# One of the last stores of a short-sequence attention kernel is cut in two, and three quarters of it are written with an outer dimension of eight

## The chip, the cores and the metric

The kernel runs on one core of a Trainium2 chip. The metric is the device time of one execution in microseconds (us); lower is better. The core has the engines PE (matmul), DVE, ACT and POOL, a queue engine SP, and 16 DMA engines that move data between the device memory and the on-chip memory (SBUF).

## The reference

32 batches with 12 heads each make 384 independent attention problems of 128 rows by 64 columns in float32:

```
scores = scale * np.matmul(q, k.transpose(0, 1, 3, 2))
scores_max = np.max(scores, axis=-1, keepdims=True)
attn = np.exp(scores - scores_max)
attn = attn / (np.sum(attn, axis=-1, keepdims=True) + 1e-8)
return np.matmul(attn, v).astype(np.float32)
```

Each of q, k, v and the output is 12.58 MB.

## The kernel before

The work goes in 24 chunks (`NCH`), numbered 0 to 23, of 16 heads each. A chunk of the output is a tile `o_sb` of 128 partitions, and each partition holds 16 rows (`TQ`) of 64 columns (`D`), that is 1024 floats or 4096 bytes that also lie together in the device memory. A whole chunk is 512 KB. Because a partition is one run of 4096 bytes on both sides, a store of a chunk consists of 128 packets of 4096 bytes; spread over 16 DMA engines that is eight packets, 32 KB, for each engine.

Loads of q, k and v are issued on POOL (lines 58 and 65) and change float32 to bfloat16 on the way, `AHEAD` = 7 chunks ahead of their use. Only chunk 0 of q and k is loaded by SP and ACT and cast by DVE and ACT (lines 78 to 84). For every chunk, in the loop at lines 210 to 229, DVE turns q and k (`turn`), PE makes the scores and ACT their exponentials (`scores`), PE makes the row sums (`denominators`), DVE turns them and takes the reciprocals (`divide`), PE multiplies with v and DVE turns the result into `o_sb` (`outputs`, `finish`), and POOL multiplies with the reciprocals (`scale_rows`, line 183; for the last chunk POOL and DVE take one half each, line 186).

Stores are held back: `held` (lines 194 to 199) is a list, written out by hand, of the chunks that are stored at the end of each step. With `LAG` = 9, chunk c is stored in step c + 9 in the middle of the run. At the end the lists get longer: step 22 stores chunks 18, 19 and 20, and step 23 stores chunks 21, 22 and 23. `store` (lines 189 to 191) is one DMA. Chunks 0 to 20 are issued from ACT's queue, chunks 21 to 23 from SP's queue (line 229). So chunk 20, which the change touches, is the last store that ACT issues, behind those of chunks 18 and 19, and three more stores follow it on SP.

Semaphores and waits are put in by the framework; they are not in the source. Among them are waits of a store for the landing of an earlier store.

Of the kernel before, what the change touches and what calls it, by code (L numbers as in the profile page):

```python
# [10 lines left out]
def kernel(  # L11
# [15 lines left out]
    B, H, S, D = q.shape  # L27
    assert S == 128 and D == 64
    scale = 1.0 / (D ** 0.5)
    TQ = 16  # L30
# [4 lines left out]
    NCH = B * H // 16  # L35
    AHEAD = 7
    LAG = 9

    def runs(x, t):
        return x.rearrange("b h (g t) d -> (b h g) (t d)", t=t).rearrange(  # L40
            "(n p) x -> p n x", p=128)

    qr, kr, vr, orr = runs(q, TQ), runs(k, TQ), runs(v, T), runs(out, TQ)
# [5 lines left out]
    pf = ctx.enter_context(tc.tile_pool(name="pf", bufs=8))  # L49
    po = ctx.enter_context(tc.tile_pool(name="po", bufs=LAG + 3))  # L50
    ps = ctx.enter_context(tc.tile_pool(name="ps", bufs=1, space=bass.MemoryType.PSUM))
# [17 lines left out]
    with tc.manual_schedule():  # L69
# [8 lines left out]
        for src, which, eng, cast in ((qr, 0, nc.sync, nc.vector.tensor_copy),  # L78
# [3 lines left out]
            x = pin.tile([128, TQ, D], bf16, tag="qk"[which] + "_bf", name="qk"[which] + "_bf")  # L82
# [105 lines left out]

        def store(c, eng):
            o_sb, _ = osbs.pop(c)  # L190
            eng.dma_start(out=orr[:, c, :], in_=o_sb.rearrange("p t d -> p (t d)"))

        e = NCH - 1
        held = {c: [c - LAG] if c >= LAG else [] for c in range(e - 4)}
        held[e - 4] = [e - 13, e - 12]
# [14 lines left out]
        for c in range(NCH):  # L210
            todo = shuffles.get(c, [])
            if c < e:
                turn(c + 1, 0)
                turn(c + 1, 1)
            d_ps = denominators(c)
            if c < e:
                scores(c + 1)
            divide(c, d_ps)
            finish(c, 0, outputs(c, 0))
            for x in todo[:len(todo) // 2]:  # L220
                values(*x)
            finish(c, 1, outputs(c, 1))
            for x in todo[len(todo) // 2:]:
                values(*x)
            if c + AHEAD < NCH:
                load(c + AHEAD)
            scale_rows(c)
            for s in held[c]:
                store(s, nc.scalar if s < e - 2 else nc.sync)
# [30 lines left out]
```

## Time and profile before

| | |
|---|---|
| three runs | 130.41, 130.43, 130.69 us, median 130.43 |
| the profiled execution | 130.47 us |
| its span, from the first to the last instruction | 128.6 us |
| busy share of the span: PE, DVE, ACT, POOL | 54%, 67%, 56%, 62% |
| DMA share of the chain that ended last | 58% |
| memory read and written | 37.75 MB and 12.58 MB |
| stores issued by ACT and by SP | 21 and 3, of 512 KB each |

The span leaves out 1.9 us of the profiled execution that lie before the first and after the last instruction. "DMA share" is the mean busy share of the 16 DMA engines in a stretch of time, in which neighbouring packets may overlap a little, so that a full stretch reads as slightly more than 1; 0.50 is what eight busy engines of 16 give. GB/s counts bytes as the packets record them: the casting loads count by what they write, half of what they read.

### The profile page before, as it was taken

How to read it: one execution, taken by the hardware profiler on the slowest of the kernel's cores; microseconds unless marked ns; L12 is line 12 of the kernel's file. 1: busy time of each engine (PE TensorE's matmuls, PEld its weight loads, DVE VectorE, ACT ScalarE, POOL GpSimd, SP SyncE). 2: the span in 40 equal slices, each digit the busy share in tenths (PEclk: the TensorE clock that was granted, in tenths of full speed). 3: DMA queues.
4: the chain of work that ended last, by engine and by line, in shares of the span. 5: the costliest groups of instructions: out<-in, count | busy, mean ns of one | idle time of the engine just before them, and what ended most of it. 6: DMA issues, size and time to landing. Idle time of an engine off the chain costs nothing.

```text
span 128.6 us, 4637 instructions
## 1 busy us (share of the span) xinstructions
PE 69.7 (54%) x2080; PEld 42.7 (33%) x2080; DVE 85.7 (67%) x150; ACT 71.8 (56%) x74; POOL 79.5 (62%) x88
## 2 busy tenths in 40 slices
PE   0036966577546757775636296190976663684000
PEld 0025644444223433443314144050544331552000
DVE  0380398584879678979958669464799997777500
ACT  3216588669658737875774486371757775523000
POOL 6951314235699986998738487808999952355300
PEclk9999999999999977999999959968689998555555
DMA  3999999999999999999999999999999999999982
GB/s 118 312 194 186 210 204 204 209 213 202 216 202 209 207 215 206 207 212 209 283 290 269 221 284 207 286 287 209 287 210 285 287 285 325 389 418 414 419 364 83
DMA packets 16723, 32.27 MB, mean 251 GB/s; under 512 B 1344, under 2 KB 7488, under 8 KB 16704
## 3 DMA queue, kind: packets, MB, share of 16 engines
q0 software_dynamic: 12960, 18.35, 80.1%
q10 hardware_dynamic: 3168, 11.54, 23.0%
q1 hardware_dynamic: 576, 2.10, 4.2%
q8 instruction: 16, 0.26, 0.7%
q14 instruction: 3, 0.02, 0.0%
HBM read 37.75 MB, written 12.58 MB: 391 GB/s over the span
## 4 chain that ended last, share of the span: by engine, by line
DMA 58%; DVE 12%; POOL 11%; PE 6%; issue 4%; ACT 1%; POOLq 0%; DVEq 0%; ACTq 0%
DMA k_bf<-in_k_dram 33%; DMA q_bf<-in_q_dram 11%; DMA v_bf<-in_v_dram 11%; DVE o_sb L178 6%; POOL o_sb L183 4%; POOL v_bf L65 4%; PE s_ps L120 3%; DMA out_dram<-o_sb 3%; DVE kt L109 3%; DVE qt L107 2%; POOL q_bf L58 2%; PE o_ps L159 2%; ACT attn L124 1%; DVE o_sb L186 1%; PE v_ps L139 1%
## 5 line engine op out<-in xcount | busy, mean ns | idle before, releaser
L124 ACT ACTIVATE attn<-s_ps 128x2048 bf16<-128x2048 f32 x24 | 45.1, 1877 | 38.2 <-PE s_ps L120 33.2
L183 POOL TENSOR_TENSOR o_sb<-o_sb,recip 128x1024 f32<-128x1024 f32 x23 | 43.9, 1915 | 8.7 <-DVE o_sb L178 8.5
L178 DVE STREAM_TRANSPOSE o_sb<-o_ps 128x512 f32<-128x512 f32 x48 | 33.1, 711 | 14.3 <-PE o_ps L159 13.2
L139 PE MATMUL v_ps<-v_bf,perm 128*32 128x512 bf16 (+1 forms) x448 | 33.5, 405 | 3.4 <-DMA v_bf<-in_v_dram 3.4
L120 PE MATMUL s_ps<-qt,kt 32*128 32x128 bf16 x768 | 17.2, 232 | 33.1 <-DVE kt L109 33.1
L143 ACT CAST v<-v_ps 128x512 bf16<-128x512 f32 x48 | 26.4, 589 | 2.6 <-PE v_ps L139 2.4
L120 PEld LDWEIGHTS <-kt 32*128 32x128 bf16 x768 | 12.6, 100 | 43.1 <-DVE kt L109 42.5
L159 PE MATMUL o_ps<-attn,v 128*32 128x128 bf16 x768 | 22.4, 245 | 2.7 <-issue 2.7
L58 POOL DMA_DIRECT2D k_bf<-in_k_dram x23 | 12.3, 536 | 15.5 <-DMA v_bf<-in_v_dram 10.8
L171 DVE STREAM_TRANSPOSE dt<-d_ps 128x512 f32<-128x512 f32 x24 | 16.3, 678 | 6.4 <-PE d_ps L149 6.4
L109 DVE STREAM_TRANSPOSE kt<-k_bf 128x512 f32<-128x512 f32 x24 | 16.3, 680 | 5.5 <-DMA k_bf<-in_k_dram 5.4
L159 PEld LDWEIGHTS <-v 128*32 128x32 bf16 x768 | 15.7, 108 | 11.4 <-issue 6.5
L58 POOL DMA_DIRECT2D q_bf<-in_q_dram x23 | 13.5, 585 | 6.4 <-DMA v_bf<-in_v_dram 3.7
L107 DVE STREAM_TRANSPOSE qt<-q_bf 128x512 f32<-128x512 f32 x24 | 16.2, 673 | 1.6 <-DMA q_bf<-in_q_dram 1.5
L149 PE MATMUL d_ps<-attn,ones 128*32 128x512 bf16 x96 | 11.4, 453 | 9.5 <-ACT attn L124 9.5
L65 POOL DMA_DIRECT2D v_bf<-in_v_dram x12 | 9.1, 760 | 9.3 <-DMA k_bf<-in_k_dram 3.4
L139 PEld LDWEIGHTS <-perm 128*32 128x32 bf16 x448 | 12.1, 110 | 5.0 <-issue 2.6
L149 PEld LDWEIGHTS <-ones 128*32 128x32 bf16 x96 | 4.7, 104 | 15.8 <-issue 12.9
L173 DVE RECIPROCAL recip<-dt 128x16 f32<-128x16 f32 x24 | 6.1, 254 | 1.9
L83 DVE CAST q_bf<-raw 128x1024 bf16<-128x1024 f32 x1 | 0.8, 815 | 5.3 <-DMA raw<-in_q_dram 5.3
L83 ACT CAST k_bf<-raw 128x1024 bf16<-128x1024 f32 x1 | 1.0, 1046 | 3.0 <-DMA raw<-in_k_dram 3.0
L83 ACT ACT_TABLE_LOAD x1 | 1.3, 1283 | 1.2 <-PEq L244 1.2
(11 smaller groups left out, 3.8 us busy)
## 6 DMA issues: line engine op xcount, KB each, us to landing
out_dram<-o_sb ACTq DMA_DIRECT2D x21, 512.0 KB, 7.4
v_bf<-in_v_dram POOLq DMA_DIRECT2D x12, 512.0 KB, 13.8
q_bf<-in_q_dram POOLq DMA_DIRECT2D x23, 256.0 KB, 13.4
k_bf<-in_k_dram POOLq DMA_DIRECT2D x23, 256.0 KB, 13.2
out_dram<-o_sb SPq DMA_DIRECT2D x3, 512.0 KB, 6.4
raw<-in_k_dram ACTq DMA_DIRECT2D x1, 512.0 KB, 4.7
raw<-in_q_dram SPq DMA_DIRECT2D x1, 512.0 KB, 4.6
```

The source lines that it names most:

```text
L58: nc.gpsimd.dma_start(out=x, in_=src[:, c, :].rearrange("p (t d) -> p t d", t=TQ))
L107: nc.vector.transpose(xt.rearrange("p h (x g) -> p x h g", g=GQ), x)
L109: nc.vector.transpose(xt.rearrange("p h (x g) -> p x h g", g=GQ), x.rearrange("p (y t) e -> p t y e", y=2))
L120: nc.tensor.matmul(s_ps[:, b, h, :], lhsT=kt[pr, h, :, j], rhs=qt[pr, h, :, j], start=(j == 0), stop=(j == 1), tile_position=(b * 32, 0))
L124: nc.scalar.activation(out=attn, in_=s_ps, func=mybir.ActivationFunctionType.Exp, bias=0.0, scale=scale)
L139: nc.tensor.matmul(v_ps[u * 32:(u + 1) * 32, i], lhsT=perm[:, a + i, tl, :], rhs=v_bf[:, ns, 2 * u + tl, :], start=(tl == 0), stop=(tl == ...
L143: nc.scalar.copy(v2s[m][:, a:a + heads, ns], v_ps)
L149: nc.tensor.matmul(d_ps[b * 32:(b + 1) * 32], lhsT=ones, rhs=attns[c][:, b], start=True, stop=True, tile_position=(0, b * 32))
L159: nc.tensor.matmul(o_ps[b * 32:(b + 1) * 32, h], lhsT=v2s[c // 4][:, 4 * (b % 2) + h, 2 * (c % 4) + b // 2, j * 32:(j + 1) * 32], rhs=attn ...
L171: nc.vector.transpose(dt, turned(d_ps))
L178: nc.vector.transpose(o_sb[:, :, j * 32:(j + 1) * 32], turned(o_ps))
L183: nc.gpsimd.tensor_mul(o_sb, o_sb, recip.to_broadcast([128, TQ, D]))
```

## The change

Chunk 20 (`NCH - 4`) is stored by two DMAs instead of one, both from ACT's queue. The first has 12 of the 16 rows of every partition, 768 floats or 3072 bytes. On the side of the device memory its 128 partitions are written as 8 groups of 16 (`"(i p) x -> i p x"` with `i=8`), so the outer dimension of that side is eight instead of 128. The side of SBUF still lists 128 partitions. The second DMA has the other 4 rows, 1024 bytes of each partition, in the old form. All other stores stay as they are.

```
+    UNEVEN = NCH - 4
...
         def store(c, eng):
             o_sb, _ = osbs.pop(c)
-            eng.dma_start(out=orr[:, c, :], in_=o_sb.rearrange("p t d -> p (t d)"))
+            if c == UNEVEN:
+                cut = 3 * TQ // 4
+                for sl in (slice(0, cut), slice(cut, TQ)):
+                    dst = orr[:, c, sl.start * D:sl.stop * D]
+                    if sl.start == 0:
+                        dst = dst.rearrange("(i p) x -> i p x", i=8)
+                    eng.dma_start(out=dst, in_=o_sb[:, sl, :].rearrange("p t d -> p (t d)"))
+            else:
+                eng.dma_start(out=orr[:, c, :], in_=o_sb.rearrange("p t d -> p (t d)"))
```

## The prediction

> **What bounds the kernel now.** I read the page first, then the stretches of the last microseconds, then the DMA queues, then the order of the stores on ACT and SP. The page's slices show the DMA engines full almost from the first to the last slice; only the last two fall.
>
> ```profile
> span 128.6 us, 4637 instructions
> ...
> DMA  3999999999999999999999999999999999999982
> ```
>
> The view of stretches looks into those last slices. Its columns are the stretch, its length, the busy time of PE, PEld, DVE, ACT and POOL with counts, the granted clock, the DMA share and GB/s.
>
> ```profile
> 118.00:120.00 2.00, 0.35 (x15) 0.08 (x4) 1.86 (x5) 0.00 (x0) 1.47 (x2) 0.50 1.02 412
> 120.00:121.00 1.00, 0.00 (x0) 0.00 (x0) 0.92 (x1) 0.00 (x0) 0.37 (x1) 0.50 1.03 418
> 121.00:122.00 1.00, 0.00 (x0) 0.00 (x0) 0.00 (x0) 0.00 (x0) 0.00 (x0) 0.50 1.01 414
> 122.00:123.00 1.00, 0.00 (x0) 0.00 (x0) 0.00 (x0) 0.00 (x0) 0.00 (x0) 0.50 1.04 426
> 123.00:124.00 1.00, 0.00 (x0) 0.00 (x0) 0.00 (x0) 0.00 (x0) 0.00 (x0) 0.50 1.02 418
> 124.00:124.50 0.50, 0.00 (x0) 0.00 (x0) 0.00 (x0) 0.00 (x0) 0.00 (x0) 0.50 0.92 377
> 124.50:125.00 0.50, 0.00 (x0) 0.00 (x0) 0.00 (x0) 0.00 (x0) 0.00 (x0) 0.50 0.71 287
> 125.00:125.50 0.50, 0.00 (x0) 0.00 (x0) 0.00 (x0) 0.00 (x0) 0.00 (x0) 0.50 0.52 213
> 125.50:126.00 0.50, 0.00 (x0) 0.00 (x0) 0.00 (x0) 0.00 (x0) 0.00 (x0) 0.50 0.48 197
> 126.00:126.50 0.50, 0.00 (x0) 0.00 (x0) 0.00 (x0) 0.00 (x0) 0.00 (x0) 0.50 0.50 205
> 126.50:127.00 0.50, 0.00 (x0) 0.00 (x0) 0.00 (x0) 0.00 (x0) 0.00 (x0) 0.50 0.21 82
> 127.00:127.50 0.50, 0.00 (x0) 0.00 (x0) 0.00 (x0) 0.00 (x0) 0.00 (x0) 0.50 0.00 0
> ```
>
> From 121 us no compute engine works, and the DMA engines drain stores. Until 124 us all 16 are busy. Then the share falls to one half, stays there for about 1.5 us, and falls to nothing before 127 us. A share that rests at 0.5 says that eight engines are done and eight are not. Taking the early eight as what lies above 0.5: (0.42 + 0.21 + 0.02) x 0.5 us x 16 / 8 = 0.65 us, so they end at 124.65 us on the mean. The late eight: 0.21 x 0.5 x 16 / 8 = 0.21 us past 126.5, so 126.71 us. The two groups are 2.06 us apart, and the late group sets the end. That is the bound: **eight DMA engines that are two microseconds behind**, not a compute engine.
>
> The cause is probably this queue on the page (packets, MB, share of 16 engines' span):
>
> ```profile
> q10 hardware_dynamic: 3168, 11.54, 23.0%
> ...
> q8 instruction: 16, 0.26, 0.7%
> ```
>
> Sixteen packets take 0.7% of 16 x 128.6 us = 14.4 us, so 0.90 us each. If they fall twice on each of eight engines, these are 1.8 us behind. Nothing in the profile gives a packet the number of its engine: **it shows that eight are late, and not which eight.** The change gives more work to a fixed eight.
>
> **The change part by part.** For the speed of one engine, the queue view of 113 to 117 us, when q10 carries nearly everything:
>
> ```profile
> q10 hardware_dynamic: 458, 1.66, 101.7%
> ```
>
> 1.66 MB are 405 packets of 4096 bytes; 1.017 x 16 x 4 us / 405 = 0.161 us each, end markers included. By the rate (418 GB/s / 16 = 26.1 GB/s for an engine) it is 0.157 us. I use 0.157.
>
> *Removed:* eight packets of 4096 bytes from each of 16 engines, 1.26 us per engine.
>
> *Added on engines 0 to 7:* 16 rows of 3072 bytes and eight of 1024, together 57,344 bytes instead of 32,768. The extra 24,576 bytes take 24,576 / 26.1 GB/s = **+0.94 us**. *On engines 8 to 15:* eight rows of 1024 bytes remain, **-0.94 us**.
>
> *Smaller packets:* what a packet costs beyond its bytes isn't shown for stores. At one end a short packet costs its bytes alone; at the other a 1024-byte one takes as long as one of 4096, +8 x 0.118 = 0.94 us per engine, and a 3072-byte one, +16 x 0.039 = 0.63 us more on engines 0 to 7. The nearest row is the load queue, in 8 to 57 us:
>
> ```profile
> DMA packets 7590, 10.11 MB, mean 206 GB/s; under 512 B 463, under 2 KB 4954, under 8 KB 7582
> ```
>
> Its packets record 1024 or 2048 bytes (twice that is read), and still it reads 2 x 206 = 412 GB/s, 1.4% under the 418 of the large packets. So the first end is nearer; I take +0.1 us for engines 0 to 7, **+1.04 us** in all, and nothing for the others.
>
> *Sharing:* each of engines 0 to 7 now presumably takes 16 neighbouring partitions instead of a spread of eight, and reads rows that engines 8 to 15 used to read. Whether two engines on neighbouring partitions slow each other no row of before shows, since all its stores have the same spread. Bounds: a row costs nothing more, or twice its time, 16 x 0.118 = +1.89 us on engines 0 to 7; a gain I exclude, since the total rate is flat at 410 to 426 GB/s. For the sum I take nothing, because that is what the flat rate of the rows is nearest to, and keep the other end as a rival.
>
> *One more DMA issue on ACT, and the waits around it:*
>
> ```profile
> L191 ACTq DMA_DIRECT2D out_dram<-o_sb x21: 338/339/1261, 57.9 to 116.2; - x21
> L191 ACTq EVENT_SEMAPHORE x14: 17/17/17, 86.7 to 116.1; - x14
> ```
>
> ```profile
> 114.62 7.63 SPq L191 DMA_DIRECT2D out_dram<-o_sb x3
> ...
> 114.95 1.88 ACT L124 ACTIVATE attn<-s_ps 128x2048 bf16<-128x2048 f32 x1 [2.32 <-DMA out_dram<-o_sb]
> 115.03 2.22 ACTq L191 DMA_DIRECT2D out_dram<-o_sb x3
> ...
> 119.82 1.10 DVE L186 TENSOR_TENSOR o_sb<-o_sb,recip 128x512 f32<-128x512 f32 x1
> ```
>
> An issue takes 0.34 to 1.26 us. ACT's last three end at 117.25, so the fourth ends by 118.5, or later if it gets a wait as 14 of the others have. Behind it on ACT nothing is queued: the last exponential is the one at 114.95. Its bytes are only needed while the engines drain a backlog that reaches to 124 us, so about 5.5 us of transfers cover it. If that cover were gone it would cost its 0.34 to 1.26 us. I cost it at nothing.
>
> *The stores of SP:*
>
> ```profile
> SPq L191 <- DMA out_dram<-o_sb: 102.5, 2, 99.8
> ```
>
> Of these two waits for the landing of an older store, the short one is 102.5 - 99.8 = 2.7 us. The three SP issues end at 114.62 + 7.63 = 122.25; the last therefore starts about 121.9, although DVE was done with chunk 23 at 120.92. So the last store already waits 1.0 us for an older landing, covered by the full engines up to 124 us. One more DMA may change which landing that is. At best nothing; if it became that of chunk 20, a store would be issued only when the drain is over, and these take 5.4 us or more to land:
>
> ```profile
> DMA to landing us min/median/max: 5.4/7.3/10.3
> ```
>
> That would be some 4 us. I take nothing.
>
> **Which way the shift acts.** The profiled execution is 130.47 us, 1.87 more than its span, and 0.04 above the median of the runs, 130.43; a change of 1 us in the end of the drain changes both alike. What counts is only where the late eight lie.
>
> *Forecast: some or all of the late engines are among 0 to 7.* Then they end 1.04 us later, 126.71 + 1.04 = 127.75 us on the mean, and the rest end earlier for no use. It is enough that one late engine is among the eight. Profiled 130.47 + 1.04 = 131.51; from the median **131.5 us**; own range 131.2 to 132.3. For it: the trace names no engine, and of all ways in which eight of 16 can lie, only one puts them all outside 0 to 7. Against it: if queues are given out in blocks, the late eight are one half or the other.
>
> *Rival 1: the late ones are exactly 8 to 15, and engines don't disturb each other.* They end at 126.71 - 0.94 = 125.77 us, the others at 124.65 + 1.04 = 125.69: nearly level. The early group ends over about 1 us, the late one over 0.5 us (rows from 124.00 and from 126.50), so the last packet moves by 0.8 to 0.94 us: **129.6 us**. For it: the steady share of 0.5, which looks like one block, and a shift that is almost exactly half of the 2.06 us.
>
> *Rival 2: the late ones are 8 to 15, but the reads of 0 to 7 disturb each other or those of the late ones.* It sits in chunk 20's first part, between about 120 and 126 us. Engines 0 to 7 have 126.71 - 125.69 = 1.02 us to spare; it decides from there, when a row takes more than 0.118 + 1.02 / 16 = 0.182 us, one and a half times its time. At twice the time they end 1.89 - 1.02 = 0.87 us after the old end: **131.3 us**; at one and a half times nothing changes. For it: eight engines then read what 16 read, and the late ones are still reading the same partitions. Against it: no row shows such a slowing.
>
> [...]
>
> *Rival 3: the change doesn't do what it says,* because the engines are chosen from the side that lists 128 partitions. Then each engine gets the old bytes in shorter packets, +0.1 us: **130.5 us**. [...]
>
> **How the numbers follow.** Forecast 0.38; rival 1 0.31; rival 2 0.21, of which 0.03 within 0.2% and 0.18 slower; rival 3 0.04; a later landing for SP's last store 0.06, slower. A measurement of this kernel can tell 0.2%, about 0.26 us, from no change. Slower: 0.38 + 0.18 + 0.06 = 0.62; same: 0.03 + 0.04 = 0.07; faster: 0.31. Both signs hold much, so the range reaches from 129.5, the low end of rival 1 (130.43 - 0.94), to 132.3, the forecast with the next 0.8 us of short packets or sharing; it leaves out the SP case and the far ends.
>
> **What the profile after would show.** Forecast: the share rests at 0.5 for 3 to 4 us instead of 1.5, to almost 128 us. Rival 1: no rest at 0.5; the share falls from 1 to 0 between about 125 and 126.2 us. Rival 2: the rate drops below 410 GB/s already before 124 us, and the rest at 0.5 is short or belongs to the other eight. Rival 3: the end looks as before. In all but rival 3 the packets rise by 136: two times 128 rows with 8 and 16 end markers make 280, against 128 with 16, 144, before. If the chain ends in an SP store issued after 123 us, the waits were moved, and the forecast is wrong for a reason that I cost at nothing.

## The result and the profile after

The changed kernel takes 130.72 us (median of 6 runs, 130.46 to 130.99), the kernel before 130.65 us beside it on the same chip (6 runs, 130.41 to 131.4). The ratio is 1.0001, 95% interval 0.9973 to 1.0029: no difference that can be measured. Forecast were 131.5 us. The profiled execution took 130.68 us with a span of 128.8 us, against 130.47 and 128.6 before. Two executions further below that ran some per cent longer than the others of their kernel, one of e2 (137.42 us) and the profiled one of e8 (135.85 us), are left out of the medians and ratios.

The first view is the page of the changed kernel, its slices and queues:

```profile
DMA  3999999999999999999999999999999999999982
...
DMA packets 16867, 32.27 MB, mean 251 GB/s; under 512 B 1360, under 2 KB 7632, under 8 KB 16848
...
q10 hardware_dynamic: 3312, 11.54, 23.1%
...
q8 instruction: 16, 0.26, 0.7%
```

The packet line of the page of before:

```profile
DMA packets 16723, 32.27 MB, mean 251 GB/s; under 512 B 1344, under 2 KB 7488, under 8 KB 16704
```

Here the reader is to count. q10 has 3312 packets against 3168, 144 more. A store of 128 rows on 16 engines is 128 data packets and 16 end markers (packets of 4 bytes; the 84 DMAs of before have 1344 of them, 16 each), 144. Two such stores instead of one are +144; a first part on eight engines, with eight markers as the DMAs of eight rows in e3 below have them, would have been +136. The column "under 512 B", in which the end markers fall, says the same by itself: 1360 - 1344 = +16, not +8. **The first part ran on 16 engines.** The trace's own record of the two instructions shows why (issue time in us, the instruction's destination, bytes of an element):

```
116.48 DMA_DIRECT2D dst_num_elem=[128,1] dst_elem_size=3072
117.65 DMA_DIRECT2D dst_num_elem=[128,1] dst_elem_size=1024
```

The destination lists 128 rows and not 8 groups of 16. The two dimensions were one again by the time the instruction was made; that they could be joined because group after group lies at the same distance as row after row is the likely reason. The trace also records when each engine's part of this DMA landed: 16 landings, eight from 121.98 to 123.58 us and eight from 125.88 to 126.81 us. The whole chunk 20 of before had 16 as well, eight from 121.91 to 123.51 and eight from 125.51 to 126.43.

The stretches at the end answer those of before (same columns):

```profile
123.00:124.00 1.00, 0.00 (x0) 0.00 (x0) 0.00 (x0) 0.00 (x0) 0.00 (x0) 0.50 1.04 425
124.00:124.50 0.50, 0.00 (x0) 0.00 (x0) 0.00 (x0) 0.00 (x0) 0.00 (x0) 0.50 1.03 418
124.50:125.00 0.50, 0.00 (x0) 0.00 (x0) 0.00 (x0) 0.00 (x0) 0.00 (x0) 0.50 0.70 283
125.00:125.50 0.50, 0.00 (x0) 0.00 (x0) 0.00 (x0) 0.00 (x0) 0.00 (x0) 0.50 0.58 238
125.50:126.00 0.50, 0.00 (x0) 0.00 (x0) 0.00 (x0) 0.00 (x0) 0.00 (x0) 0.50 0.48 193
126.00:126.50 0.50, 0.00 (x0) 0.00 (x0) 0.00 (x0) 0.00 (x0) 0.00 (x0) 0.50 0.55 221
126.50:127.00 0.50, 0.00 (x0) 0.00 (x0) 0.00 (x0) 0.00 (x0) 0.00 (x0) 0.50 0.40 150
127.00:127.50 0.50, 0.00 (x0) 0.00 (x0) 0.00 (x0) 0.00 (x0) 0.00 (x0) 0.50 0.08 25
```

The rest at 0.5 is there as before. Worked out in the prediction's way, the early eight end at 124.5 + (0.20 + 0.08) x 0.5 x 2 = 124.78 us and the late eight at 126.5 + (0.40 + 0.08) x 0.5 x 2 = 126.98 us, 2.2 us apart (before: 2.06). No work moved from one group to the other.

ACT's and SP's last stores in the order of time, and SP's waits:

```profile
114.34 7.58 SPq L200 DMA_DIRECT2D out_dram<-o_sb  x3
...
114.67 1.88 ACT L125 ACTIVATE attn<-s_ps 128x2048 bf16<-128x2048 f32 x1 [2.32 <-PE s_ps L121]
114.75 1.10 ACTq L200 DMA_DIRECT2D out_dram<-o_sb  x2
116.48 1.51 ACTq L198 DMA_DIRECT2D out_dram<-o_sb  x2
```

```profile
SPq L200 <- DMA out_dram<-o_sb: 101.6, 2, 98.9
```

The additional issue is over at 116.48 + 1.51 = 117.99 us with nothing behind it, and SP's short wait for an older landing is 101.6 - 98.9 = 2.7 us as before.

### The profile page after: what moved, and what is told of

The parts are those of the page before. It is cut to its first block, busy times and chain, and to the rows that moved or that the text cites. A ratio compares the mean times of both kernels' runs of the same rounds, so it can differ in the third digit from the quotient of the medians.

```text
span 128.8 us, 4638 instructions
## 1 busy us (share of the span) xinstructions
PE 69.3 (54%) x2080; PEld 43.1 (33%) x2080; DVE 85.6 (66%) x150; ACT 71.5 (56%) x74; POOL 79.4 (62%) x88
## 2 busy tenths in 40 slices
DMA packets 16867, 32.27 MB, mean 251 GB/s; under 512 B 1360, under 2 KB 7632, under 8 KB 16848
## 3 DMA queue, kind: packets, MB, share of 16 engines
q10 hardware_dynamic: 3312, 11.54, 23.1%
## 4 chain that ended last, share of the span: by engine, by line
DMA 55%; DVE 15%; POOL 11%; PE 7%; issue 4%; ACT 1%; POOLq 0%; DVEq 0%; ACTq 0%
DMA k_bf<-in_k_dram 33%; DMA q_bf<-in_q_dram 11%; DMA v_bf<-in_v_dram 11%; DVE o_sb L179 7%; POOL o_sb L184 4%; PE s_ps L121 4%; POOL v_bf L66 4%; DVE kt L110 3%; DVE qt L108 3%; POOL q_bf L59 2%; PE o_ps L160 2%; ACT attn L125 1%; DVE o_sb L187 1%; POOL k_bf L59 1%; DVE dt L172 1%
## 5 line engine op out<-in xcount | busy, mean ns | idle before, releaser
L121 PE MATMUL s_ps<-qt,kt 32*128 32x128 bf16 x768 | 18.1, 240 | 32.8 <-DVE kt L110 32.8
L140 PE MATMUL v_ps<-v_bf,perm 128*32 128x512 bf16 (+1 forms) x448 | 32.5, 395 | 3.7 <-DMA v_bf<-in_v_dram 3.7
L144 ACT CAST v<-v_ps 128x512 bf16<-128x512 f32 x48 | 26.1, 592 | 2.8 <-PE v_ps L140 2.8
L121 PEld LDWEIGHTS <-kt 32*128 32x128 bf16 x768 | 13.3, 104 | 41.5 <-DVE kt L110 40.9
L150 PE MATMUL d_ps<-attn,ones 128*32 128x512 bf16 x96 | 10.7, 424 | 10.4 <-ACT attn L125 10.4
```

Of the source, the lines that this page charges most:

```text
L121: nc.tensor.matmul(s_ps[:, b, h, :], lhsT=kt[pr, h, :, j], rhs=qt[pr, h, :, j], start=(j == 0), stop=(j == 1), tile_position=(b * 32, 0))
L140: nc.tensor.matmul(v_ps[u * 32:(u + 1) * 32, i], lhsT=perm[:, a + i, tl, :], rhs=v_bf[:, ns, 2 * u + tl, :], start=(tl == 0), stop=(tl == ...
L144: nc.scalar.copy(v2s[m][:, a:a + heads, ns], v_ps)
L150: nc.tensor.matmul(d_ps[b * 32:(b + 1) * 32], lhsT=ones, rhs=attns[c][:, b], start=True, stop=True, tile_position=(0, b * 32))
```

## The experiments

Theory after the result: the outer dimension of eight does nothing, and the change is only a cut of one store in two parts on 16 engines. Rival: the first part did go to fewer engines, and a loss on late engines and a gain elsewhere cancel. Behind it stand the questions that the prediction left open: what a store on few engines really does here, which engines are late, and why.

**e1_two_plain.** The two parts without the outer dimension (the lines are against the changed kernel).

```
-                    if sl.start == 0:
-                        dst = dst.rearrange("(i p) x -> i p x", i=8)
```

> Chunk 20 is stored in the same two parts, 3072 and 1024 bytes of each partition, both in the old form with 128 rows outermost. Theory A (the eight groups of 16 rows lie at even distances and become 128 rows again, so that the first part ran on all 16 engines): nothing differs from the changed kernel, 16867 packets, a rest of the DMA share at 0.5 to about 126.7 us, and a time within 0.2% of both kernels (130.4 to 130.9). Theory B (the first part did run on engines 0 to 7, and what it shifted was eaten by engines that disturb each other): fewer or more packets than the changed kernel, and an end of the drain of another shape.

Measured: 130.71 us, before 130.64, ratio 1.0006 (0.9988 to 1.0024). Its page:

```profile
DMA packets 16867, 32.27 MB, mean 251 GB/s; under 512 B 1360, under 2 KB 7632, under 8 KB 16848
```

Packet for packet the count of the changed kernel. In both traces a 3072-byte packet takes 121.1 ns on the mean and a 1024-byte one 46.0 ns, together 167 ns, against 159 ns for one of 4096 bytes in the same stretch, from 120 us on. The cut costs 8 x 8 ns = 0.06 us per engine, too little to be seen in the time.

**e9_outer_only.** Chunk 20 whole, in one DMA, with the outer dimension alone.

```
-            eng.dma_start(out=orr[:, c, :], in_=...)
+            dst = orr[:, c, :]
+            if c == NCH - 4:
+                dst = dst.rearrange("(i p) x -> i p x", i=8)
+            eng.dma_start(out=dst, in_=...)
```

> Chunk 20 is stored whole, by one DMA, and the only edit is the outer dimension of eight on the side of the device memory. Theory: groups that lie at an even distance are joined again to 128 rows before the instruction is made, so the DMA is the old one: packets 16723 with 1344 of them under 512 B as before, 21 stores of 512 KB on ACT, share resting at 0.5 to 126.5 us, time the same within 0.2% (130.4 to 130.7). Rival A: the outer dimension does choose eight engines, and in the changed kernel only the cut undid it; then 8 end markers fewer (packets 16715), 32 KB more on each of eight engines, +1.25 us on those that are late among them: about 131.9. Rival B: it chooses eight early engines: faster, at 129.5 or below.

Measured: 130.56 us, before 130.70, ratio 0.9993 (0.9973 to 1.0012). Its page has the packets of before, to the last one:

```profile
DMA packets 16723, 32.27 MB, mean 251 GB/s; under 512 B 1344, under 2 KB 7488, under 8 KB 16704
```

With e1 and the 16 landings above this settles it: the cut alone is the whole change, and the outer dimension alone is no change.

**e5_seven.** What would have happened, had the DMA gone to few engines? 119 rows are 7 x 17 and have no larger divisor up to 16. Chunk 20 at its old place in three parts (`cut` is 12 of the 16 rows, as in the changed kernel):

```
+            for rows, cols in ((slice(0, 119), slice(0, cut)), (slice(119, 128), slice(0, cut)),
+                               (slice(0, 128), slice(cut, TQ * D))):
+                eng.dma_start(out=orr[rows, c, cols], in_=flat[rows, cols])
```

> Chunk 20 at its old place on ACT, in three DMAs: 3072 bytes of 119 partitions, 3072 bytes of the other nine, 1024 bytes of all 128. If the number of engines is the largest number up to 16 that divides the outermost size, 119 = 7 x 17 goes to seven engines with 17 rows each. Seven engines then get 17 x 3072 + 3072 + 8192 = 63488 bytes instead of 32768 (plus 1.18 us at 26.1 GB/s) and the others 8192 or 11264 (minus 0.94 or 0.82 us). Theory A (the change stayed on 16 engines; shifted bytes do move the end, and the seven are not among the late ones): the rest at 0.5 goes, the late eight end 0.82 to 0.94 us earlier, time 129.5 to 129.9. Theory A with late engines among the seven: 131.3 to 131.8. Theory B (reads across the partitions disturb each other): 130.4 or more, and the rate falls below 400 GB/s before 124 us.

Measured: 131.66 us, before 130.62, ratio 1.0091 (1.0073 to 1.0109), +1.04 us. The landings of the first part in the trace are one entry at 118.03 us, as soon as it was issued, and then seven:

```
123.80 124.74 124.84 124.91 125.19 127.72 127.92
```

Seven engines, five early and two late. The end of the kernel:

```profile
122.00:123.00 1.00, 0.00 (x0) 0.00 (x0) 0.00 (x0) 0.00 (x0) 0.00 (x0) 0.50 0.93 346
123.00:124.00 1.00, 0.00 (x0) 0.00 (x0) 0.00 (x0) 0.00 (x0) 0.00 (x0) 0.50 0.99 357
...
126.00:126.50 0.50, 0.00 (x0) 0.00 (x0) 0.00 (x0) 0.00 (x0) 0.00 (x0) 0.50 0.40 160
126.50:127.00 0.50, 0.00 (x0) 0.00 (x0) 0.00 (x0) 0.00 (x0) 0.00 (x0) 0.50 0.25 102
127.00:127.50 0.50, 0.00 (x0) 0.00 (x0) 0.00 (x0) 0.00 (x0) 0.00 (x0) 0.50 0.21 84
127.50:128.00 0.50, 0.00 (x0) 0.00 (x0) 0.00 (x0) 0.00 (x0) 0.00 (x0) 0.50 0.13 45
```

At 26.1 GB/s for one engine (418 / 16), 84 and 45 GB/s are the last two or three. The forecast's sum, made for these engines, needs one row more: the DMA of the other nine rows has nine landings, seven of them within 0.5 us after the seven above, the last two at 128.13 and 128.32 us, which reads as the same seven engines and two others. That makes 18 x 0.121 + 8 x 0.046 - 8 x 0.159 = +1.27 us. The measured 1.04 us is of this size; that it equals the forecast's 1.04 us to the last digit is chance, since the terms differ. Two other things show here. The rate falls to 346 and 357 GB/s while 119 partitions are read by seven engines; e1 in the same stretch, 122 to 124 us, keeps its rate (first line e5, second e1):

```profile
DMA packets 231, 0.70 MB, mean 352 GB/s; under 512 B 15, under 2 KB 54, under 8 KB 231
```

```profile
DMA packets 267, 0.84 MB, mean 419 GB/s; under 512 B 25, under 2 KB 66, under 8 KB 267
```

And the 3072-byte packets take 135.5 ns on the mean instead of 121.1: most still take 121 ns, but eleven of the 128 take 171 to 554 ns, all between 121.8 and 124.2 us. So something slows packets here. By what, and whether neighbouring partitions have to do with it, isn't shown: which partitions each engine reads is in no trace.

**e8_seven_twice.** The same for chunks 19 and 20.

```
-            if c == NCH - 4:
+            if c in (NCH - 5, NCH - 4):
```

> As e5_seven, but chunk 19 is cut in the same way too, so the shift is doubled: seven engines get 2.35 us more and most others 1.88 us less. Theory A with the late ones outside the seven: the seven are now the last, at about 124.65 + 2.35 = 127.0 us on the mean instead of the late eight at 126.7, so the time is 130.5 to 131.2, above e5_seven, and the share rests near 0.44. With late engines among the seven: 132.5 or more. If neither cut moves the end: as the kernel before.

Measured: 133.39 us (three runs), before 130.62, ratio 1.0208 (1.0191 to 1.0226): +2.8 us, more than twice e5. ACT's six issues of these two chunks need 11 us in its trace, but that trace is of the execution of 135.85 us. How much of the 2.8 us belongs to the engines' load and how much to issues and waits isn't separated.

**e2_eight_spread, e3_eight_bunched, e4_sixteen.** Eight engines can be had by DMAs of eight partitions (e3's page has 1440 packets under 512 B against 1344, 96 or 12 x 8 end markers more). Chunk 12, issued on SP in 12 of them and one of 32 partitions; e2 with every twelfth partition, e3 with eight neighbours, e4 as a control with 16 partitions and half of the columns (16 engines: 1536 packets under 512 B, 12 x 16 more than the 1344).

```
+                for j in range(12):
+                    rows = slice(j, 96, 12)             # e2; e3: slice(8 * j, 8 * j + 8)
+                    nc.sync.dma_start(out=orr[rows, c, :], in_=flat[rows, :])
+                    # e4: rows 16 * (j // 2) on, 16 of them, columns 512 * (j % 2) on, 512 of them
+                nc.sync.dma_start(out=orr[96:, c, :], in_=flat[96:, :])
```

> Chunk 12 goes by SP in 12 DMAs of eight partitions each (12 partitions apart), 4096 bytes per partition, and one of the last 32 partitions. If a DMA with eight rows outermost runs on eight engines, and always the same, these get 14 rows and the others 2 instead of 8 each: plus and minus 24576 bytes, 0.94 us. Theory A with the late engines outside these eight: about 129.6 us, no rest of the share at 0.5. Theory A with late engines among them: 131.4 us, the rest at 0.5 lasts over 3 us. Theory B (reads across the partitions disturb each other): no gain or a loss, and packets on SP's queue that take clearly longer than 0.16 us.

> As e2_eight_spread, but each of the 12 DMAs takes eight neighbouring partitions. If engines that read neighbouring partitions disturb each other, packets on SP's queue take up to four times as long as in e2_eight_spread, and the time is up to 2 us above it; if not, the two are equal within 0.3 us.

> The control for e2_eight_spread: the same 13 DMAs on SP with the same bytes, but each of the 12 has 16 neighbouring partitions with half of their columns, so that all 16 engines get the same. If the shift between engines is what counts, this is as the kernel before (130.4 to 130.7), with the rest of the share at 0.5; if the number of DMAs or the issue by SP counts, it moves as e2_eight_spread does.

Measured: e2 131.18 us (nine runs), ratio 1.0031 (1.0012 to 1.005); e3 131.3, ratio 1.0046 (1.0031 to 1.0062); e4 132.49, ratio 1.0149 (1.0111 to 1.0186); before 130.64. SP issued them as soon as chunk 12 was ready, from 83 us on, among the loads. In their traces what lies behind came later; SP's stores and the last exponential of e2, and of e4:

```profile
83.45 8.95 SPq L196 DMA_DIRECT2D out_dram<-o_sb  x12
...
116.51 6.69 SPq L199 DMA_DIRECT2D out_dram<-o_sb  x3
```

```profile
116.89 1.88 ACT L125 ACTIVATE attn<-s_ps 128x2048 bf16<-128x2048 f32 x1 [2.32 <-PE s_ps L121]
```

```profile
118.64 1.88 ACT L125 ACTIVATE attn<-s_ps 128x2048 bf16<-128x2048 f32 x1 [2.32 <-DMA out_dram<-o_sb]
```

That exponential stood at 114.95 us before. Single traces scatter, though: in e9, as fast as before, it starts at 115.89 us, and in e12 below, where nothing is changed ahead of it, at 117.00. So only e4's delay is clearly more than scatter. e4, with no uneven engines at all, is the slowest, 1.85 us above before: 13 early stores have a price of their own, and the difference of e2 to e4 (131.18 and 132.49 us) isn't the price of uneven engines. As a measure of the load these runs fail. What they still show: in the last stretches of e2

```profile
126.00:126.50 0.50, 0.00 (x0) 0.00 (x0) 0.00 (x0) 0.00 (x0) 0.00 (x0) 0.50 0.31 123
126.50:127.00 0.50, 0.00 (x0) 0.00 (x0) 0.00 (x0) 0.00 (x0) 0.00 (x0) 0.50 0.14 57
127.00:127.50 0.50, 0.00 (x0) 0.00 (x0) 0.00 (x0) 0.00 (x0) 0.00 (x0) 0.50 0.14 57
```

the rest at 0.5 is gone, and 57 GB/s, two engines, are left over; the last store's landings end with two at 128.16 and 128.41 us, 1.2 us behind the other 14. As in e5, two late ones are among those that got more. And e3 equals e2 within their intervals: eight neighbours a DMA, one packet for each engine, show no disturbance in the time, and a 4096-byte packet on SP's queue between 83 and 93 us takes 172 ns at the median in both. The "up to four times as long" of the expectation was the author's estimate; no run shows it.

**e6_eight_late, e7_sixteen_late.** The same with chunk 20 on SP, e7 being the control (the line is against e2).

```
-            if c in UNEVEN:          # chunk 12
+            if c == NCH - 4:
```

> Chunk 20 goes by SP, as soon as its data is there at about 110.4 us, in 12 DMAs of eight partitions each (12 partitions apart) and one of 32 partitions; so unlike e2_eight_spread the shift falls into the drain and delays no load. Theory A with the late engines outside these eight: 129.5 to 130.0, unless 13 issues with their waits hold up SP's later stores, and clearly below e7_sixteen_late. Theory B or late engines among the eight: not below e7_sixteen_late.

> The control for e6_eight_late: 13 DMAs at the same place, of which 12 have 16 partitions and half the columns, so that all engines get the same bytes. Theory A: as the kernel before (130.4 to 130.9) with a rest at 0.5. If the place or the number of DMAs counts and not the engines: as e6_eight_late.

Measured: e6 131.59 us, ratio 1.0072 (1.0053 to 1.0091); e7 132.4, ratio 1.0146 (1.012 to 1.0172); before 130.62. SP of e6 in order of time, then its DMA rate:

```profile
110.95 11.11 SPq L195 DMA_DIRECT2D out_dram<-o_sb  x12
...
122.67 1.89 SPq L198 DMA_DIRECT2D out_dram<-o_sb  x3
```

```profile
122.00:124.00 2.00, 0.00 (x0) 0.00 (x0) 1.69 (x2) 0.00 (x0) 1.05 (x1) 0.50 0.78 272
124.00:126.00 2.00, 0.00 (x0) 0.00 (x0) 0.00 (x0) 0.00 (x0) 0.00 (x0) 0.50 1.02 410
```

Twelve issues with their waits for older landings hold SP for 11 us; the stores of chunks 21 to 23 start after them, and the engines run short of work at 122 to 124 us. Again the control is slower than the case, so these two are inconclusive on the load. But e7 shows something else: its engines are full and yet move little.

```profile
120.00:121.00 1.00, 1.00 (x36) 0.82 (x28) 0.66 (x1) 0.00 (x0) 0.00 (x0) 0.50 0.97 334
121.00:122.00 1.00, 0.14 (x8) 0.00 (x0) 0.90 (x4) 0.00 (x0) 0.00 (x0) 0.50 0.97 242
```

Its 2048-byte packets take 84 ns at the median and 124 on the mean; 48 of the 192 take more than 1.15 times 84. Each of its twelve DMAs has 16 neighbouring partitions and, as the same DMAs in e4 show by their 12 x 16 end markers, runs on all 16 engines, so the loss seen in e5 is not bound to few engines. In e4, the same DMAs among the loads, the mean is 97 ns and the median 96: there it is absent.

**e10_half_pe.** Why are eight engines late? The instruction packets were only probable. Half of PE's instructions left out:

```
-                for j in range(2):        # scores
+                for j in range(1):
-                for tl in range(2):       # values
+                for tl in range(1):
-            finish(c, 0, outputs(c, 0))
+            o_ps = outputs(c, 0)
+            finish(c, 0, o_ps)
+            finish(c, 1, o_ps)
...
-            finish(c, 1, outputs(c, 1))
```

> Stores as before. About half of PE's instructions are left out: the second half of the contraction in the scores, half of the reordering of v, and the outputs of the upper 32 columns, which are copies of the lower ones; 2176 PE instructions remain of 4160. All loads, stores and the other engines' work stay. Theory: the eight late engines are late because each moved two of the 16 instruction packets of 16 KB, at 0.9 us a packet; 2176 instructions make 8 packets, one for each of the eight, so the rest of the share at 0.5 lasts about 1 us instead of 2, and the end comes 0.9 to 1.0 us earlier: 129.5 to 129.8. Rival A: the eight engines are late for another reason (something fixed, like the casting loads): the rest at 0.5 stays 2 us long and the time is the same within 0.2%. Rival B: PE's work bounds the kernel somewhere after all: more than 1.3 us faster, with a DMA share that is higher in the middle.

Measured: 129.59 us, before 130.70, ratio 0.9907 (0.9877 to 0.9938). Its queue and its end:

```profile
q8 instruction: 8, 0.13, 0.4%
```

```profile
124.00:124.50 0.50, 0.00 (x0) 0.00 (x0) 0.00 (x0) 0.00 (x0) 0.00 (x0) 0.50 0.82 336
124.50:125.00 0.50, 0.00 (x0) 0.00 (x0) 0.00 (x0) 0.00 (x0) 0.00 (x0) 0.50 0.64 262
125.00:125.50 0.50, 0.00 (x0) 0.00 (x0) 0.00 (x0) 0.00 (x0) 0.00 (x0) 0.50 0.37 148
125.50:126.00 0.50, 0.00 (x0) 0.00 (x0) 0.00 (x0) 0.00 (x0) 0.00 (x0) 0.50 0.06 25
```

Eight packets instead of 16. The early group ends at 124 + (0.32 + 0.14) x 0.5 x 2 = 124.46 us, the late one at 125 + (0.37 + 0.06) x 0.5 x 2 = 125.43: a gap of 0.97 us instead of 2.06, while the early group moves by only 0.19. That fits one packet of about 0.9 us per late engine instead of two; the 0.19 us are a gain from elsewhere, and the gap alone is put down to the packets. Their times repeat after eight, too: before has 935, 974, 974, 961, 893, 893, 949, 945 ns and then 994, 975, 974, 964, 893, 893, 942, 931, and e10 has one such round, 974, 961, 892, 893, 1001, 945, 935, 960. That is what eight engines that take turns would give. So the instruction packets are PE's, 16 of them with all its instructions and 8 with half, and by the gap of 2.06 and 0.97 us they go through the eight late engines and make the last microsecond of the kernel.

**e11_map.** Which engines? Chunk 20 on ACT in DMAs of 1, 2, 3, 4, 6 and 112 partitions.

```
+                lo = 0
+                for n in (1, 2, 3, 4, 6, 112):
+                    eng.dma_start(out=orr[lo:lo + n, c, :], in_=flat[lo:lo + n, :])
+                    lo += n
```

> A map of the engines, not a candidate. Chunk 20 is stored at its old place on ACT in six DMAs of 1, 2, 3, 4, 6 and 112 partitions with all their columns. Each small DMA puts one packet of 4096 bytes on each of as many engines, behind whatever these still have to do, so its landings show whether they are early or late. Theory: of the seven engines of the DMA of 119 partitions two are late, and these landed about 2.5 us after the others; so the landings of the small DMAs split as well, and the smallest DMA that has a landing late by about 2 us tells how many engines can be given more work without touching a late one. [...] Rival: the split in two was made by that DMA itself; then all landings of one small DMA lie within 0.5 us. Time: four or five issues more on ACT, 0.34 to 1.4 us each, covered until about 124 us; six packets more on the engine that all six DMAs use and 112/16 = 7 instead of 8 on all, so +0.8 us if the first engine is late (131.4), as before or 0.15 us less if not. [...]

Measured, one run of each: 131.25 us, before 130.74. Landings in the trace (us), those of chunk 19, issued just ahead, with its early eight and late eight, and the small ones:

```
chunk 19  120.95 to 122.35, 123.40 to 123.87
1 row     121.13
2 rows    121.31 121.88
3 rows    121.50 121.73 122.06
4 rows    122.98 123.07 123.12 123.44
6 rows    126.43 126.47 126.54 126.63 126.78 127.05
```

The DMAs of 1, 2 and 3 rows land with the early eight, the four of the fourth lie within 0.5 us. Taken in the order of issue, as the late eight of before land chunks 18, 19 and 20 from 121.76, 123.47 and 125.51 us on, a late engine could land its row only behind its part of chunk 19, so after 123.40 us and one packet more, 123.56. So the engines of the DMAs of up to four rows are early, with all their landings by 123.44 us. That all six DMAs use one engine, on which the expected time rests, isn't shown: the trace gives no engine numbers. The DMA of 6 says nothing: it was issued only at 125.06 us, after a wait for the landing of one of SP's stores, when the queues were nearly empty. That wait, and the 112 rows behind it, explain the time.

**e12_four.** The version that this points to: more work for four early engines.

```
+                cut = 6 * D
+                for rows, cols in ((slice(0, 116), slice(0, cut)), (slice(116, 128), slice(0, cut)),
+                                   (slice(0, 128), slice(cut, TQ * D))):
+                    eng.dma_start(out=orr[rows, c, cols], in_=flat[rows, cols])
```

> The version that the map points to. Chunk 20 goes in three DMAs: 116 partitions with 1536 bytes each (116 = 4 x 29, so four engines, all of them early by the map), the other 12 partitions with 1536 bytes (12 engines), and 2560 bytes of all 128 partitions. By the durations of earlier runs (9 ns a packet and 36.6 ns a KB; 159 ns for 4096 bytes) a late engine has 8 x 0.1005 + 0.065 = 0.87 us of work here instead of 1.27, so it ends 0.40 us earlier, and each of the four early engines 1.48 us more, from 124.65 to 126.13 us on the mean, still before the late ones at 126.31. Theory: 0.3 to 0.4 us faster than before, ratio 0.997, the last rest of the share at about 12/16 and shorter than in before. Rival A: reads across the partitions disturb each other as in the DMA of seven engines, at about 14 ns a row of 29 and more; then the four end level with the old end: same within 0.2%. Rival B: the split between early and late in the map was made by the order of landing alone; then four late engines end 1.5 us later: about 131.9.

Measured: 130.94 us (130.11 to 131.86, 12 runs), before 130.69, ratio 1.0021 (0.9998 to 1.0044): not faster, and with a spread about four times that of before (1.75 against 0.45 us). The four landings of the first part, 124.64, 124.71, 124.83 and 125.26 us, lie close together, so the map was right and rival B falls. Where the forecast's gain went shows only in part. Its profiled execution (131.73 us, at the upper end of the runs) lags before the change acts: chunk 20 is issued from 118.44 us on, and by 118 us 28.86 MB had moved, against 29.09 in before, which is 0.55 us at 418 GB/s. After that the rate falls too:

```profile
121.00:122.00 1.00, 0.00 (x0) 0.00 (x0) 0.97 (x3) 0.00 (x0) 0.63 (x1) 0.50 1.01 367
122.00:123.00 1.00, 0.00 (x0) 0.00 (x0) 0.96 (x1) 0.00 (x0) 0.41 (x1) 0.50 0.90 286
123.00:124.00 1.00, 0.00 (x0) 0.00 (x0) 0.00 (x0) 0.00 (x0) 0.00 (x0) 0.50 1.02 378
```

against 414 to 426 GB/s before, and its 1536-byte packets take 101.9 ns on the mean where the undisturbed ones take 65 (30 of 128 are over 1.15 times that). The last store's landings end with four at 127.99, 128.06, 128.30 and 128.61 us, behind the other twelve, which end at 127.42: presumably the four that got more are now the last. This is rival A, with a higher price than written, in this execution; of the faster ones there is no trace. No version here that does the whole work beats both kernels.

## Why the prediction was wrong

**What bounds the kernel: right,** and the guess about the cause too. Eight engines are about 2 us behind at the end (2.06 us with 16 instruction packets, 0.97 with eight in e10), as two packets of about 0.9 us each would make them.

**The step that failed** is "*Added on engines 0 to 7*", with "*On engines 8 to 15*" beside it, and so the sentence "The change gives more work to a fixed eight". Both took the words of the diff for what the DMA does. No run shows that eight groups of 16 rows put a DMA on engines 0 to 7, or on any eight: the first part had 16 landings, and e9, with the outer dimension alone, 1344 packets under 512 B as before. Each of 16 engines kept its old bytes; +1.04 and -0.94 us were terms of a transfer that doesn't exist in the changed kernel. Forecast, rival 1 and rival 2 all stood on it, with 0.90 together. That 130.72 us lies within the stated 129.5 to 132.3 us speaks for none of them: the range joins a loss and a gain, and neither came.

**Rival 3 happened,** held at 0.04: 130.5 us forecast, 130.72 measured, at a before that came out at 130.65 this time. Its effect was put rightly, the same bytes per engine in shorter packets; its reason was not. The side of SBUF didn't outvote eight groups; the destination itself carried 128 rows (`dst_num_elem=[128,1]`, the record above), and the 16 end markers show 16 engines. The slip was to read the number of engines off the source text. By their landings, other DMAs of this case had seven engines for 119 rows (e5), four for 116 (e12) and three for three (e11).

**Shorter packets:** +0.1 us taken, 0.06 us for each engine by the packets' times (e1).

**The issue on ACT and SP's waits:** costed at nothing, and nothing it was; the issue ends at 117.99 us, inside the 118.5 that were given.

**"It is enough that one late engine is among the eight":** right where it could be tried. e5 on seven engines caught two late ones and became 1.04 us slower. The guess of rivals 1 and 2 that the late ones are exactly the eight that a DMA on eight engines leaves out falls too: the eight of e2 include two of them, as the seven of 119 rows do. The traces give no engine numbers, and how the other six lie was not mapped.

**Sharing, taken as nothing:** it would have been wrong for a DMA like those of e5 and e12. The flat 410 to 426 GB/s came from stores that were all of one form and could not show it. In e5 a row takes 135.5 instead of 121.1 ns on the mean, in e12 101.9 instead of 65; e7 loses likewise on 16 engines (124 ns on the mean, 84 at the median), and the packet times of e3 (172 ns, as in e2) and e4 (97 on the mean, 96 at the median) show hardly any of it. What makes the difference stays open.

**The signs:** the packets decided, as written: 136 more in all but rival 3, and it was 144.

## What to carry to other kernels

In these runs the number of engines that a DMA gets followed the dimensions in the instruction, not those in the source: here a split at an even distance was joined again, and `[128,1]` went to 16 engines. Count end markers, or look at the destination in the trace, before a price is put on engines; and when a prediction hangs on one premise about what the code becomes, give the case that it doesn't a chance that fits, since all other cases fall with it. At an end that only DMA engines drain, ask what else these engines carry (here PE's instructions, in 16 packets of about 0.9 us), and look whether moving bytes to a few of them costs rate, as it did in e5 (346 GB/s) and e12 (286) against 414 to 426 in before.

## What the runs showed of the hardware

- An instruction packet of 16 KB took 0.89 to 0.99 us in before. With 16 of them eight engines ended 2.06 us behind the other eight, with 8 of them 0.97 us (e10), as two and one packets for each would give. Halving PE's instructions made a kernel with the same loads and stores 0.9% faster (e10).
- By the landings two of the seven engines of 119 rows are late (127.72 and 127.92 us, the other five by 125.19, e5), and so are two engines in e2 (128.16 and 128.41 us); the engines of the DMAs of up to four rows are all early (landings by 123.44 us, e11).
- From 120 us on, with no loads beside it, a store packet took 46, 65, 102, 121 and 159 ns at the median for 1024, 1536, 2560, 3072 and 4096 bytes (1024 and 3072 in the changed kernel, 1536 and 2560 in e12, 4096 in before): about 9 ns and 37 ns for each KB. Among the loads, between 57 and 83 us, one of 4096 bytes took 172 ns in before.
- Stores can lose rate while the engines read as full: 242 GB/s at a share of 0.97 in e7 from 121 to 122 us, 346 at 0.93 in e5 from 122 to 123, against 414 to 426 in before.
- A DMA issue took 0.34 us alone (ACT in before and in the changed kernel), but 12 small ones in a row held SP for 11.11 us (e6), and ACT's fifth small DMA of e11 came 4.3 us after the fourth, for a wait on an older landing.
